# Five up-projection pairs per FFN layer in seven-product blocks, three down chunks of six, and retimed scheduler costs, in a two-layer hybrid decoder trunk

## The chip, the core and the metric

One NeuronCore of a Trainium2 chip runs the whole program. The metric is device time in microseconds of one execution; the time of a kernel is the median over its runs. TensorE is written PE, VectorE DVE, ScalarE ACT, GpSimd POOL, SyncE SP.

## What is computed

The trunk has two layers over 512 tokens of width 1024, all in float32. Layer 0 mixes with a Mamba-2 scan and a stick-breaking attention, layer 1 with an mLSTM; each layer then adds a gated convolutional FFN. The change is almost wholly in that FFN:

```python
def conv_ffn(h, up_w, conv_w, conv_b, down_w):
    u = causal_dwconv(h @ up_w, conv_w, conv_b)
    gate, val = jnp.split(u, 2, axis=-1)
    return (jax.nn.silu(gate) * val) @ down_w
...
        h = h + conv_ffn(rmsnorm(h, norm_w[layer, 1]), ffn_up_w[layer], ffn_conv_w[layer],
                         ffn_conv_b[layer], ffn_down_w[layer])
```

`up_w` is 1024 x 5632 (22 tiles of 128 gate columns, 22 of value columns), `down_w` is 2816 x 1024.

## The kernel before

Activations lie transposed, features on the 128 partitions and 512 tokens along the free axis: eight tiles of the residual `h`, each in a slot of a pool of 71 equal slots on chip. Every float32 product is made of three float32r products (`mm3`): each operand is split in a rounded part `hi` and a remainder `lo`, and hi*hi, hi*lo and lo*hi are summed in PSUM. ACT makes `hi` (a cast) and DVE makes `lo` (a subtraction), for the activations (`split`) and for every weight as it comes in from memory (`split_weights`). SP loads weights in "units" into two `raw` buffers; the split units stand in five `hi`/`lo` pairs (`W_BUFS`), so the makers of a unit wait until PE is done with the unit five before.

In `ffn` (line 1174) the step `("up", j)` is a pair: gate tile j and value tile 22+j. Each is eight weight tiles against eight token tiles (`feat`), 24 matmuls of 512 columns; then DVE scales by the norm (`u`), ACT and DVE make the three taps of the convolution (`c`), ACT the SiLU, DVE the product.

The down projection of the first 16 tiles is done by `down_blocks` (line 1227) in seven block products instead of eight (a Strassen-Winograd scheme on 2x2 blocks: two feature tiles by two halves of the tokens). For a pair of feature tiles, `token_sums` makes the token-side combinations (11, 21, 22, n1, n2, t3, t4) on DVE and splits them. On the weight side a block unit (`weight_tiles`) reads four blocks: the first two raw; two combinations `P1` and `P3` by a load from SP onto which a second DMA, issued by POOL, adds another block in flight; `P2` and `P4` by additions on DVE; the last raw. Seven products of 256 token columns run in three PSUM banks X, Z, Y, and DVE adds each finished partial sum to `h`, seven reads of 128x256 per pair of output tiles. The order is `FFN_PLAN`: chunks of eight tiles (`CHUNKS`) once their ups are done, and the last six tiles (`REST`) by plain products in `down_rest`.

The order of instructions is not the order of the code. All calls are recorded, and `Recorder.order` (line 318) makes a list schedule from them: each call has a cost in ns (`cost`), each pair of engines a latency, and pools of slots and buffers hold a call back until the right earlier tile is free. Each engine then runs its list strictly in turn. A cost thus changes no instruction, but which stands ahead of which, in the whole program.

Of the kernel before, what the change touches and what calls it, by code (L numbers as in the profile page):

```python
# [15 lines left out]
F32 = mybir.dt.float32  # L16
# [6 lines left out]
P = 128  # L23
# [61 lines left out]
def _ffn_units(i, l):  # L85
# [3 lines left out]
    for kind, n in FFN_PLAN:  # L89
        if kind == "up":  # L90
# [6 lines left out]
        else:  # L97
# [175 lines left out]
class Recorder:  # L273
# [15 lines left out]
    def cost(c):  # L289
# [25 lines left out]
        return 60 + 2.0 * n  # L315
# [129 lines left out]
SLOTS = 71  # L445
# [3 lines left out]
class Net:  # L449
# [724 lines left out]
    def ffn(self, l, h, last):  # L1174
        nc = self.nc
        xs, _, _, rb = self.norm(h, f"nw{l}1")
        pairs, ss, first = {}, [], None
        for kind, j in FFN_PLAN:
            if kind == "down":
                a, b = CHUNKS[j]  # L1180
                for c in range(4):
                    self.down_blocks([pairs[k] for k in range(a // 2, b // 2)], h, c)
# [4 lines left out]
            cc = []  # L1187
            for part in range(2):
                n = j + part * FF
                ps = self.ps(("pj", "zz", "yy")[self.n % 3])  # L1190
                self.feat(ps, xs)
                u, c = self.slot("u"), self.slot("c")
                nc.vector.tensor_tensor(u, ps, rb, op=ALU.mult)
                nc.scalar.activation(c, u, AF.Identity, scale=self.param(f"fw{l}2", n), bias=self.param(f"fb{l}", n))
                for d in (1, 2):
                    nc.vector.scalar_tensor_tensor(c[:, d:T], u[:, 0 : T - d], self.param(f"fw{l}{2 - d}", n), c[:, d:T],
                                                   op0=ALU.mult, op1=ALU.add)
                cc.append(c)
            nc.scalar.activation(cc[0], cc[0], AF.Silu)
            nc.vector.tensor_tensor(cc[1], cc[0], cc[1], op=ALU.mult)  # L1200
# [7 lines left out]
    def token_sums(self, c1, c2):  # L1208
# [275 lines left out]
```

## Time and profile before

| what | us |
|---|---|
| median of 3 runs (1389.22 to 1389.76) | 1389.6 |
| the profiled execution | 1389.56 |
| its span, first to last instruction | 1387.8 |
| PE busy | 1376.7 (99%) |
| DVE busy | 1116.2 (80%) |
| ACT busy | 783.9 (56%) |
| POOL busy | 87.1 (6%) |

Layer 0's FFN runs from about 452 to 808 us of the span, layer 1's from about 1027 to the end. A busy share of PE counts overlapped, modelled ends of its matmuls; how far apart they start is read from the chain of waits, where a run of n matmuls on the path has a length.

### The profile page before, as it was taken

The numbers are of one execution on the slowest core, as the hardware profiler recorded it, in microseconds if no ns is written. First come the engines' busy times: TensorE is split into PE (matmuls) and PEld (weight loads), VectorE is DVE, ScalarE is ACT, GpSimd is POOL, SyncE is SP. The second block draws the span as 40 slices with busy tenths as digits, with TensorE's granted clock in tenths as the row PEclk, the third lists the DMA queues.
The fourth block names the chain that finished last, engine by engine and source line by source line (L and its number), as shares of the span: only waits on it lengthen the run. The fifth ranks groups of instructions, "written<-read, shape, count | busy, mean of one in ns | idle before, by whom it ended". The sixth has DMA issues, their size and how long they took to land.

```text
span 1387.8 us, 20206 instructions
## 1 busy us (share of the span) xinstructions
PE 1376.7 (99%) x7491; PEld 1185.3 (85%) x7491; DVE 1116.2 (80%) x1963; ACT 783.9 (56%) x1325; POOL 87.1 (6%) x172
## 2 busy tenths in 40 slices
PE   9999999999999999999999999999999999999998
PEld 8898998989788888988898898888888899889887
DVE  7999889999997778878877657798758886888662
ACT  7798997786665444344434446776434444444440
POOL 0000001201120001000100000110000010010000
PEclk9999999999999999999999999999999999999999
DMA  6423223223312345243532225222234354443422
GB/s 220 130 77 112 86 78 98 70 83 132 98 46 91 101 127 137 92 138 113 129 122 95 81 82 171 77 92 89 65 106 126 102 129 129 122 133 95 137 68 84
DMA packets 53617, 147.96 MB, mean 107 GB/s; under 512 B 6136, under 2 KB 7160, under 8 KB 53520
## 3 DMA queue, kind: packets, MB, share of 16 engines
q1 hardware_dynamic: 48912, 138.29, 31.4%
q0 software_dynamic: 4608, 8.39, 3.7%
q8 instruction: 59, 0.97, 0.3%
q14 instruction: 38, 0.31, 0.1%
HBM read 141.36 MB, written 2.15 MB: 103 GB/s over the span
## 4 chain that ended last, share of the span: by engine, by line
PE 88%; DVE 5%; issue 3%; ACT 3%; POOL 1%; DMA 0%; SPq 0%; DVEq 0%; POOLq 0%; ACTq 0%
PE pj L436 43%; PE yy L436 26%; PE zz L436 14%; PE tt L436 5%; DVE gt L436 1%; DVE wt L436 1%; DVE lo L436 1%; DVE wTl L436 0%; ACT L436 0%; ACT Kh L436 0%; DMA h<-in_xT 0%; POOL wt L436 0%; ACT Q L436 0%; DVE ss L436 0%; ACT hi L436 0%
## 5 line engine op out<-in xcount | busy, mean ns | idle before, releaser
L436 ACT CAST hi<-raw 128x1024 fp32r<-128x1024 f32 (+2 forms) x236 | 227.8, 968 | 257.2 <-PE yy L436 58.6
L436 DVE TENSOR_TENSOR lo<-raw,hi 128x1024 fp32r<-128x1024 f32 (+2 forms) x236 | 263.8, 1120 | 25.2 <-ACT hi L436 24.5
L436 PE MATMUL pj<-xnh,hi 128*128 128x512 f32 x488 | 194.1, 398 | 0.0
L436 PE MATMUL pj<-xnh,lo 128*128 128x512 f32 x488 | 193.9, 397 | 0.0
L436 PE MATMUL pj<-xnl,hi 128*128 128x512 f32 x488 | 193.5, 396 | 0.0
L436 DVE SCALAR_TENSOR_TENSOR c<-u,pp,c 128x511 f32<-128x511 f32 (+2 forms) x212 | 158.0, 748 | 3.9 <-ACT c L436 1.6
L436 PE MATMUL yy<-xnl,hi 128*128 128x512 f32 x320 | 126.4, 395 | 0.0
L436 PE MATMUL yy<-xnh,lo 128*128 128x512 f32 x320 | 126.2, 394 | 0.0
L436 PE MATMUL yy<-xnh,hi 128*128 128x512 f32 x320 | 125.6, 392 | 0.0
L436 PE MATMUL pj<-lo,xnh 128*128 128x384 f32 (+2 forms) x320 | 108.6, 340 | 0.0
L436 PEld LDWEIGHTS pj<-xnh,lo 128*128 128x128 f32 x488 | 91.8, 188 | 19.1
L436 PEld LDWEIGHTS pj<-xnl,hi 128*128 128x128 f32 x488 | 91.8, 188 | 18.9
L436 PEld LDWEIGHTS pj<-xnh,hi 128*128 128x128 f32 x488 | 91.9, 188 | 18.8 <-issue 0.2
L436 PE MATMUL pj<-hi,xnl 128*128 128x384 f32 (+2 forms) x320 | 107.2, 336 | 0.0
L436 PE MATMUL pj<-hi,xnh 128*128 128x384 f32 (+2 forms) x320 | 106.8, 338 | 0.0
L436 ACT ACTIVATE c<-u,pp 128x512 f32<-128x512 f32 x100 | 81.1, 813 | 9.7 <-DVE u L436 8.3
L436 PE MATMUL zz<-xnl,hi 128*128 128x512 f32 x184 | 72.7, 395 | 0.0
L436 PE MATMUL zz<-xnh,lo 128*128 128x512 f32 x184 | 72.5, 394 | 0.0
L436 PE MATMUL zz<-xnh,hi 128*128 128x512 f32 x184 | 72.2, 392 | 0.0
L436 PEld LDWEIGHTS yy<-xnh,hi 128*128 128x128 f32 x320 | 60.2, 188 | 14.0
L436 PEld LDWEIGHTS yy<-xnl,hi 128*128 128x128 f32 x320 | 60.1, 188 | 13.9
L436 PEld LDWEIGHTS yy<-xnh,lo 128*128 128x128 f32 x320 | 60.1, 188 | 13.3
(418 smaller groups left out, 3330.7 us busy)
## 6 DMA issues: line engine op xcount, KB each, us to landing
raw<-in_w SPq DMA_DIRECT2D x168, 512.0 KB, 3.4
raw<-in_w SPq DMA_DIRECT2D x44, 384.0 KB, 3.1
P<-in_w SPq DMA_DIRECT2D x32, 256.0 KB, 5.6
P<-in_w POOLq DMA_DIRECT2D x32, 256.0 KB, 6.8
h<-in_xT SPq DMA_DIRECT2D x16, 256.0 KB, 4.7
E<-acsd SPq DMA_DIRECT2D x16, 256.0 KB, 3.9
raw<-in_w SPq DMA_DIRECT2D x16, 256.0 KB, 3.1
raw<-in_w SPq DMA_DIRECT2D x8, 264.0 KB, 2.7
```

Source lines behind the costliest of these rows:

```text
L436: getattr(getattr(nc, c.engine), c.method)(*(r(a) for a in c.args), **{k: r(v) for k, v in c.kw.items()})
```

## The change

Each FFN layer makes ups 7, 10, 13, 16 and 19 with the seven-product scheme: the two output tiles are gate and value tile, the four inner block pairs are the eight feature tiles of the normed input. The token-side combinations of the input (`xb`) are made once per layer, in four steps `("x", k)` between the first ups, from `h` times the norm weight (`hw`). The seven products per block (`blocks`, shared with the down projection) are gathered from PSUM to `u1` and `u2` by ACT (four of seven) and DVE (three), and then scaled. The down chunks are three of six tiles, with `REST` 18. There are 72 slots instead of 71. The scheduler's costs are changed for PE's products, DVE's scans, POOL's powers and masks. `SLOT` and all other constants stand.

```diff
-        if kind == "up":
+        if kind == "up" and n in UP_BLOCKS:
+            u.append(np.stack([up[m][:, k::2] for m in (n, FF + n) for k in range(2)], axis=1))
...
-CHUNKS = [(0, 8), (8, 16)]
-REST = 16
-FFN_PLAN = [("up", j) for j in range(9)] + [("down", 0)] + [("up", j) for j in range(9, 17)] + [("down", 1)]
-FFN_PLAN += [("up", j) for j in range(17, FF)] + [("rest", 0)]
+
+CHUNKS = [(0, 6), (6, 12), (12, 18)]
+REST = 18
+UP_BLOCKS = (7, 10, 13, 16, 19)
+FFN_PLAN = [("up", 0), ("up", 1), ("x", 0), ("up", 2), ("x", 1), ("up", 3), ("x", 2), ("up", 4), ("x", 3), ("up", 5)]
+FFN_PLAN += [("up", 6), ("down", 0)] + [("up", j) for j in range(7, 12)]
+FFN_PLAN += [("up", 12), ("down", 1)] + [("up", j) for j in range(13, 18)]
+FFN_PLAN += [("up", 18), ("down", 2)] + [("up", j) for j in range(19, FF)] + [("rest", 0)]
...
-                return max(n / 2.4 + 2.5, m * 0.84)
-            return max(4 * n / 2.4 + 5, 3.4 * m)
+                return max(n * 0.4414 + 5, m * 0.84)
+            return max(4 * n * 0.4414 + 5, 3.4 * m)
         if c.engine == "vector":
             rate = 0.52 if c.method == "tensor_scalar" and not psum else 1.042
             if c.method == "reciprocal":
                 rate = 6.2
+            if c.method == "tensor_tensor_scan":
+                rate = 2.04
...
-        return 60 + 2.0 * n
+        if c.method == "tensor_tensor":
+            return 250 + 190 * n
+        return 330 + 0.6 * n if c.method == "affine_select" else 100
...
-SLOTS = 71
+SLOTS = 72
...
-            r1, r2 = self.raw_tile(), self.raw_tile()[:, 0:kb]
+            r1, r2 = self.raw_tile()[:, 0 : 2 * kb], self.raw_tile()[:, 0:kb]
             self.nc.sync.dma_start(r1, src[:, 0 : 2 * kb])
-            p1, p2, p3, p4 = (self.slot(f"P{k}") for k in (1, 2, 3, 4))
+            p1, p2, p3, p4 = (self.slot(f"P{k}", n=kb) for k in (1, 2, 3, 4))
...
+            if kind == "x":
+                hw = []
+                for k in (2 * j, 2 * j + 1):
+                    hw.append(self.slot("hw"))
+                    v.tensor_scalar(hw[-1], h[k], self.param(f"nw{l}1", k), None, op0=ALU.mult)
+                xb.append(self.token_sums(*hw, xs[2 * j], xs[2 * j + 1]))
+                continue
...
+            us, cc = [None, None], []
+            if j in UP_BLOCKS:
+                us = self.up_blocks(xb, rb, j)
...
+                n, u, c = j + part * FF, us[part], self.slot("c")
+                if u is None:
+                    ps = self.ps(("pj", "zz", "yy")[self.n % 3])
+                    self.feat(ps, xs)
+                    u = self.slot("u")
+                    v.tensor_tensor(u, ps, rb, op=ALU.mult)
...
+    def token_sums(self, c1, c2, s1=None, s2=None):
...
+        half = lambda t, s: (t[0][:, s], t[1][:, s])
+        if s1 is None:
+            t = self.slot("B11", F32R)
+            self.nc.scalar.copy(t[:, a], c1[:, a])
+            v.tensor_tensor(t[:, b], c1[:, a], t[:, a].bitcast(F32), op=ALU.subtract)
+            s11, s2 = (t[:, a], t[:, b]), self.split(c2, "s")
+        else:
+            s11 = half(s1, a)
...
+    def blocks(self, xs, c, read):
...
         kb, n = len(xs) * P, T // 2
...
+        steps = (X, "11", "X1"), (Z, "21", "Z"), (X, "n2", "X2"), (Y, "n1", "Y1"), (X, "t3", "X3"), (Y, "22", "Y2"), (X, "t4", "X4")
+        for i, (ps, form, name) in enumerate(steps):
...
+    def up_blocks(self, xs, rb, c):
+        nc, v = self.nc, self.nc.vector
+        a, b = slice(0, T // 2), slice(T // 2, T)
+        u1, u2 = self.slot("u"), self.slot("u")
+        def read(name, ps):
+            if name in ("X1", "X2"):
+                nc.scalar.copy(u1[:, a if name == "X1" else b], ps)
+            elif name in ("Y1", "X4"):
+                nc.scalar.activation(u2[:, b if name == "Y1" else a], ps, AF.Copy, scale=-1.0)
+            elif name == "X3":
+                v.tensor_tensor(u2[:, b], u2[:, b], ps, op=ALU.subtract)
+            else:
+                o = u1[:, a if name == "Z" else b]
+                v.tensor_tensor(o, o, ps, op=ALU.add)
+        self.blocks(xs, c, read)
+        for u in (u1, u2):
+            v.tensor_tensor(u, u, rb, op=ALU.mult)
+        return u1, u2```

Three places in the instruction lists. On PE, where layer 0 reaches the end of the first down chunk (names: `F`, `s`, `G` the token-side forms of the FFN's activations, `xnh`/`xnl` the split input, `hi`/`lo` a weight unit; the number tells tiles apart). Before, PE goes from the down products to an ordinary up of 512 columns:

```order
L436 MATMUL pj_6638<-sh_6168,hi_6539 128x256
L436 MATMUL pj_6638<-sl_6181,hi_6539 128x256
L436 MATMUL pj_6638<-sh_6168,lo_6550 128x256
L436 MATMUL yy_6686<-xnh_5207,hi_6599 128x512
L436 MATMUL yy_6686<-xnl_5240,hi_6599 128x512
```

Of the change, it goes to up 7, of 256 columns:

```order
L446 MATMUL pj_6459<-Fh_6057,hi_6354 128x256
L446 MATMUL pj_6459<-Fl_6072,hi_6354 128x256
L446 MATMUL pj_6459<-Fh_6057,lo_6379 128x256
L446 MATMUL yy_6489<-xnh_5200,hi_6441 128x256
L446 MATMUL yy_6489<-xnl_5232,hi_6441 128x256
L446 MATMUL yy_6489<-xnh_5200,lo_6468 128x256
```

The first product of up 7 ("11") takes the split input itself and stands between products of the down chunk.

On DVE, the norm ahead of layer 0's FFN, from the remainder of the sum of squares (`accl`) to the first `u`. Before:

```order
L436 TENSOR_TENSOR accl_5438<-acc_5220,acch_5429 128x512
L436 TENSOR_TENSOR lo_5446<-raw_5401,hi_5435 128x1024
L436 TENSOR_SCALAR var_5457<-tt_5441 128x4
L436 COPY rep_5467<-rstd_5463 128x512
L436 TENSOR_TENSOR u_5489<-pj_5387,rb_5481 128x512
```

Of the change:

```order
L446 TENSOR_TENSOR accl_5465<-acc_5213,acch_5454 128x512
L446 TENSOR_SCALAR hw_5473<-h_4054,pp 128x512
L446 TENSOR_TENSOR lo_5481<-raw_5402,hi_5467 128x1024
L446 TENSOR_SCALAR var_5491<-tt_5463 128x4
L446 TENSOR_TENSOR Gl_5493<-G_5457,Gh_5477 128x512
L446 TENSOR_SCALAR hw_5502<-h_4064,pp 128x512
L446 TENSOR_TENSOR F_5505<-hw_5473 128x256
L446 SCALAR_TENSOR_TENSOR F_5505<-hw_5502,F_5505 128x256
L446 COPY rep_5512<-rstd_5498 128x512
L446 TENSOR_TENSOR Fl_5526<-F_5505,Fh_5515 128x512
L446 TENSOR_TENSOR u_5538<-zz_5415,rb_5529 128x512
```

The token-side sums of the input now stand between the variance, its power on POOL (`rstd`) and the first use of the norm.

On SP, and on DVE which waits for it, the loads of the `P` tiles. Before, around the first down chunk of layer 0:

```order
L436 DMA P_1276_5700<-in_w 128x512
L436 DMA P_1278_5706<-in_w 128x512
L436 DMA raw_5738<-in_w 128x1024
L436 DMA raw_5776<-in_w 128x1024
L436 DMA raw_5830<-in_w 128x1024
L436 DMA raw_5867<-in_w 128x1024
L436 DMA raw_5912<-in_w 128x1024
L436 DMA raw_5949<-in_w 128x1024
```

Of the change, around the third chunk of layer 0:

```order
L446 DMA raw_8176<-in_w 128x768
L446 DMA P_1684_8211<-in_w 128x384
L446 DMA P_1686_8233<-in_w 128x384
L446 DMA raw_8246<-in_w 128x384
L446 DMA P_1701_8257<-in_w 128x384
L446 DMA P_1703_8314<-in_w 128x384
L446 DMA raw_8357<-in_w 128x768
L446 DMA P_1718_8372<-in_w 128x384
```

Before, this unit's P loads stood six raw loads ahead of its own first raw load (raw_5949); now they stand right behind it (raw_8176 belongs with P_1684 and P_1686), and the next unit's follow. On DVE, the stretch that ends with the addition that needs P_1684; of the change:

```order
L446 TENSOR_TENSOR Fl_8224<-F_8157,Fh_8215 128x512
L446 SCALAR_TENSOR_TENSOR G_8202<-F_8157,c_8171 128x256
L446 SCALAR_TENSOR_TENSOR c_8221<-u_8209,pp,c_8221 128x511
L446 TENSOR_TENSOR lo_8240<-raw_8089,hi_8207 128x384
L446 SCALAR_TENSOR_TENSOR c_8221<-u_8209,pp,c_8221 128x510
L446 TENSOR_TENSOR Gl_8251<-G_8202,Gh_8236 128x512
L446 TENSOR_TENSOR u_8268<-zz_8204,rb_5529 128x512
L446 TENSOR_TENSOR lo_8275<-raw_8176,hi_8260 128x768
L446 TENSOR_TENSOR h_4016<-h_4016,pj_8262 128x256
L446 SCALAR_TENSOR_TENSOR c_8281<-u_8268,pp,c_8281 128x511
L446 TENSOR_TENSOR P_1685_8312<-P_1684_8211,raw_8176 128x384
```

The numbers of tiles rise in the order in which the list schedule takes calls up, so a load numbered 8211 is taken up while DVE stands between u_8209 and P_1685_8312; before, 44 instructions of DVE lay between P_1276_5700 and the addition that reads it (P_1277_6016).

## Rows read from the trace of the kernel before

**Rows 1.** The page, busy time of each engine: busy us, share of the span, instructions.
```profile
PE 1376.7 (99%) x7491; PEld 1185.3 (85%) x7491; DVE 1116.2 (80%) x1963; ACT 783.9 (56%) x1325; POOL 87.1 (6%) x172
```

**Rows 2.** Chain that ended last, whole span: start us, us, what, matmuls in the piece.
```profile
462.99 73.59 PE pj L436 x318
...
561.56 1.42 PE zz L436 x12
...
732.94 11.11 PE yy L436 x48
...
789.86 4.16 PE tt L436 x18
```

**Rows 3.** Busy time by stretch, both FFNs and the mixers of both layers.
```profile
core 0: us, PE busy (x) PEld busy (x) DVE busy (x) ACT busy (x) POOL busy (x), PEclk, DMA share, GB/s
200.00:420.00 220.00, 216.30 (x1266) 189.65 (x1264) 207.13 (x391) 158.67 (x310) 36.27 (x65) 1.00 0.28 85
...
452.00:808.00 356.00, 356.00 (x1874) 304.20 (x1873) 276.31 (x420) 159.11 (x223) 16.52 (x41) 1.00 0.39 112
...
812.00:1030.00 218.00, 216.57 (x1162) 182.80 (x1161) 166.80 (x373) 128.37 (x250) 15.99 (x41) 1.00 0.32 101
1027.00:1387.00 360.00, 357.16 (x1878) 304.77 (x1877) 266.05 (x405) 147.25 (x204) 15.30 (x17) 1.00 0.38 112
```

**Rows 4.** Waits, whole span: engine, line, waited for, us, times, longest us.
```profile
ACT hi L436 <- PE yy L436: 71.1, 47, 3.8
```

**Rows 5.** DVE in order of time, two idle times of layer 0's FFN.
```profile
461.23 0.43 DVE L436 COPY rep<-rstd 128x512 f32<-128x512 f32 x1 [1.12 <-POOL rstd L436]
...
598.79 0.69 DVE L436 TENSOR_TENSOR u<-yy,rb 128x512 f32<-128x512 f32 x1 [2.52 <-PE yy L436]
```

**Rows 6.** DVE, 452 to 808 us, groups by form: busy us, mean ns, idle before.
```profile
L436 DVE TENSOR_TENSOR lo<-raw,hi 128x1024 fp32r<-128x1024 f32 x48 | 58.7, 1222 | 7.0 <-ACT hi L436 7.0
...
L436 DVE TENSOR_TENSOR lo<-P,hi 128x512 fp32r<-128x512 f32 x32 | 21.7, 687 | 2.0 <-ACT hi L436 1.9
...
L436 DVE TENSOR_TENSOR u<-pj,rb 128x512 f32<-128x512 f32 x21 | 14.5, 691 | 19.3 <-PE pj L436 17.2 <-ACT rb L436 2.0
...
L436 DVE TENSOR_TENSOR h<-h,pj 128x256 f32<-128x256 f32 x28 | 11.7, 419 | 6.7 <-PE pj L436 6.1
...
L436 DVE TENSOR_TENSOR lo<-raw,hi 128x768 fp32r<-128x768 f32 x8 | 7.6, 956 | 0.1
```

**Rows 7.** DVE in order of time, 480 to 485 us: start us, us, instruction.
```profile
480.26 0.42 DVE L436 TENSOR_TENSOR G<-c,c 128x256 f32<-128x256 f32 x1
480.60 0.42 DVE L436 SCALAR_TENSOR_TENSOR G<-F,c 128x256 f32<-128x256 f32 x1
...
482.13 1.22 DVE L436 TENSOR_TENSOR lo<-raw,hi 128x1024 fp32r<-128x1024 f32 x1
483.27 0.69 DVE L436 TENSOR_TENSOR Fl<-F,Fh 128x512 fp32r<-128x512 f32 x1
483.87 0.69 DVE L436 TENSOR_TENSOR Gl<-G,Gh 128x512 fp32r<-128x512 f32 x1
```

**Rows 8.** ACT, 452 to 808 us, groups by form.
```profile
L436 ACT CAST hi<-raw 128x1024 fp32r<-128x1024 f32 x48 | 50.5, 1051 | 68.9 <-PE yy L436 27.9 <-PE pj L436 22.4 <-DMA raw<-in_w 15.6
...
L436 ACT CAST hi<-P 128x512 fp32r<-128x512 f32 x32 | 18.8, 617 | 23.1 <-PE pj L436 7.3 <-PE yy L436 7.2 <-issue 6.2
...
L436 ACT CAST B<-c 128x256 fp32r<-128x256 f32 x8 | 3.2, 402 | 7.0 <-DVE c L436 7.0
```

**Rows 9.** DMA issues, 452 to 808 us: KB each, median us from issue to landing.
```profile
raw<-in_w SPq DMA_DIRECT2D x47, 512.0 KB, 3.4
P<-in_w SPq DMA_DIRECT2D x16, 256.0 KB, 5.3
P<-in_w POOLq DMA_DIRECT2D x16, 256.0 KB, 6.6
```

**Rows 10.** PE, whole span, groups by form: busy us, mean ns of one.
```profile
L436 PE MATMUL pj<-xnh,hi 128*128 128x512 f32 x488 | 194.1, 398 | 0.0
...
L436 PE MATMUL pj<-Fh,hi 128*128 128x256 f32 x64 | 18.1, 282 | 0.0
```

More of the change, by code (lines that the diff above doesn't have):

```diff
@@ L96, in _ffn_units @@
             u += [x.reshape(P, 4, (b - a) // 2, P) for x in t]
-        else:
+        elif kind == "rest":
             u += _feat(dn[REST * P :])
     return u
-CHUNKS = [(0, 8), (8, 16)]
-REST = 16
-FFN_PLAN = [("up", j) for j in range(9)] + [("down", 0)] + [("up", j) for j in range(9, 17)] + [("down", 1)]
-FFN_PLAN += [("up", j) for j in range(17, FF)] + [("rest", 0)]
+CHUNKS = [(0, 6), (6, 12), (12, 18)]
[5 more added lines that the diff above has]
+FFN_PLAN += [("up", 18), ("down", 2)] + [("up", j) for j in range(19, FF)] + [("rest", 0)]
 X = lambda kind, *ns: [(kind, n) for n in ns]
@@ L1174, in ffn @@
     def ffn(self, l, h, last):
-        nc = self.nc
+        nc, v = self.nc, self.nc.vector
         xs, _, _, rb = self.norm(h, f"nw{l}1")
-        pairs, ss, first = {}, [], None
+        pairs, ss, first, xb = {}, [], None, []
         for kind, j in FFN_PLAN:
+            if kind == "x":
[5 more added lines that the diff above has]
+                continue
             if kind == "down":
@@ L1181, in ffn @@
                 for c in range(4):
-                    self.down_blocks([pairs[k] for k in range(a // 2, b // 2)], h, c)
+                    self.down_blocks([pairs[k] for k in range(a // 2, b // 2)], h[2 * c], h[2 * c + 1], c)
                 continue
@@ L1222, in token_sums @@
         gs = self.split(g, "G")
-        half = lambda t, s: (t[0][:, s], t[1][:, s])
-        return {"11": (t[:, a], t[:, b]), "21": half(s2, a), "22": half(s2, b),
+        return {"11": s11, "21": half(s2, a), "22": half(s2, b),
                 "n1": half(fs, a), "n2": half(fs, b), "t3": half(gs, a), "t4": half(gs, b)}
-    def down_blocks(self, xs, h, c):
-        v = self.nc.vector
+    def blocks(self, xs, c, read):
         kb, n = len(xs) * P, T // 2
-        a, b = slice(0, n), slice(n, T)
         X, Z, Y = (self.ps(t)[:, 0:n] for t in (("pj", "yy", "zz"), ("yy", "pj", "pj"))[c % 2])
-        h1, h2 = h[2 * c], h[2 * c + 1]
-        at = {"i": 0, "u": None}
-        def product(ps, form, more=False):
-            i = at["i"]
+        steps = (X, "11", "X1"), (Z, "21", "Z"), (X, "n2", "X2"), (Y, "n1", "Y1"), (X, "t3", "X3"), (Y, "22", "Y2"), (X, "t4", "X4")
+        for i, (ps, form, name) in enumerate(steps):
             if i % 2 == 0:
-                at["u"] = self.unit()
-            hi, lo = at["u"]
-            at["i"] = i + 1
+                hi, lo = self.unit()
+            more = name[1:] > "1"
             for k, x in enumerate(xs):
@@ L1247, in product, with down_blocks, read @@
                 self.mm3(ps, (hi[:, s], lo[:, s]), x[form], not more and k == 0, k == len(xs) - 1, skip_group_check=more)
-        add = lambda o, ps, op=ALU.add: v.tensor_tensor(o, o, ps, op=op)
-        product(X, "11")
-        product(Z, "21")
-        add(h1[:, a], X)
-        product(X, "n2", True)
-        add(h1[:, a], Z)
-        product(Y, "n1")
-        add(h1[:, b], X)
-        product(X, "t3", True)
-        add(h2[:, b], Y, ALU.subtract)
-        product(Y, "22", True)
-        add(h2[:, b], X, ALU.subtract)
-        product(X, "t4", True)
-        add(h1[:, b], Y)
-        add(h2[:, a], X, ALU.subtract)
+            read(name, ps)
+    def down_blocks(self, xs, h1, h2, c):
+        a, b = slice(0, T // 2), slice(T // 2, T)
+        to = {"X1": h1[:, a], "Z": h1[:, a], "X2": h1[:, b], "Y2": h1[:, b], "Y1": h2[:, b], "X3": h2[:, b], "X4": h2[:, a]}
+        def read(name, ps):
+            op = ALU.add if name in ("X1", "Z", "X2", "Y2") else ALU.subtract
+            self.nc.vector.tensor_tensor(to[name], to[name], ps, op=op)
+        self.blocks(xs, c, read)
+    def up_blocks(self, xs, rb, c):
+        nc, v = self.nc, self.nc.vector
+        a, b = slice(0, T // 2), slice(T // 2, T)
+        u1, u2 = self.slot("u"), self.slot("u")
+        def read(name, ps):
+            if name in ("X1", "X2"):
[7 more added lines that the diff above has]
+                v.tensor_tensor(o, o, ps, op=ALU.add)
+        self.blocks(xs, c, read)
+        for u in (u1, u2):
+            v.tensor_tensor(u, u, rb, op=ALU.mult)
+        return u1, u2
     def down_rest(self, ss, h, last):
         nc = self.nc
-        for c in range(8):
+        for c in range(KD):
             ps = self.ps(("pj", "zz", "yy", "tt")[c % 4])
```

18 lines of the change are left out of this document (4 added, 14 removed).

## Prediction

> **What bounds the kernel now.** First the busy times: PE 99%, DVE 80%, ACT 56% [rows 1]. PE's number alone proves little, since overlapped matmuls count as busy; so next the chain of waits, for the pace at which matmuls start [rows 2]. In the FFN 318 matmuls of 512 columns take 73.59 us and 48 take 11.11, which is 0.2314 us each; 12 of 256 columns take 1.42, or 0.1183. Now the whole of a layer's FFN by this pace: 22 pairs x 48 x 0.2314 = 244.4; eight down blocks x 84 x 0.1183 = 79.5; eight rests of 4.16 = 33.3 [rows 2]; 357.2 in all. The stage takes about 356 [rows 3]. So in the FFN PE never waits, and matmul work taken away there is time taken away, as long as the makers keep up. They do so with room: DVE is busy 276.3 of 356 us, ACT 159.1 [rows 3], and the casts of weights wait for PE to free a buffer [rows 4], as DVE waits for finished products (2.5 us in one case [rows 5]). The mixers have little idle PE: 3.7 us and 1.4 us in two stretches that hold them [rows 3]. The granted clock is 1.00 in each stretch, which is the level of 2.4 GHz, and an FFN as dense as before gives no cause for another.
>
> **PE, the gain.** A pair done plainly costs 48 x 0.2314 = 11.11; in blocks 7 products x 4 blocks x 3 = 84 matmuls of 256 columns, 9.94. That is 1.17 less. Per layer five up pairs and, since the chunks cover 18 tiles instead of 16, one more down pair (84 small ones for 48 large over the four output pairs): 6 x 1.17 = 7.0; two layers: 14.0. All of it lies on the path. The number of weight loads rises by 36 per pair, 432 in all, but the pace of 0.1183 was measured with a load before each matmul.
>
> A rule that speaks against this: the Trainium skill, "TensorE: Matmul & The Clock Gate", section Back-to-back issue gap, gives a sustained 131 ns per matmul at 512 columns and 81 ns at 128. By it a half-width matmul costs much more than half, and an estimate of some 98 ns at 256 makes a block pair 8.2 us against 6.3 plain, so the change would lose near 2 us per pair; the rows here, 231 and 118 ns for float32r, do not bear it out.
>
> **DVE, what is added.** The durations of DVE's groups [rows 6] overlap by some 0.085 us; what an instruction occupies is read from start to start [rows 7]: 0.60 for 512 columns (483.27 to 483.87), 1.14 for 1024, 0.34 for 256; by the same overlap 0.87 for 768 [rows 6] and 0.47 for 384, between its neighbours.
> Up pair in blocks: the splits become 1.14 + 5 x 0.60 = 4.14 instead of 2 x 1.14 = 2.28; two additions for P2 and P4, 1.20; three reads of PSUM, 1.01; the scaling stays at two of 0.60. +4.1, five times: +20.4.
> Input forms: four steps of two `hw`, four half-width sums and two remainders: 4 x (0.68 + 1.36 + 1.20) = +13.0. For `hw` no row shows the operation; the nearest are the one-input copy of 512 columns at 0.43 less overlap [rows 5] and a two-input one at 0.60, so 0.34 to 0.60; I take 0.34, as it has one tensor operand; the other end adds 2.
> Down: a block is 0.87 + 5 x 0.47 + 2 x 0.47 + 7 x 0.34 = 6.5, twelve of them 78; before 1.14 + 7 x 0.60 + 2.35 = 7.7, eight of them 61.5: +16.5. Rest: eight splits of 512 for 768, -2.2. One more pair in token sums, 3.5 for 1.2: +2.3.
> Sum +50 per layer: 326 of an FFN that would last 349. ACT [rows 8] gains some 30: a block pair 1.05 + 5 x 0.62 + 4 x 0.40 = 5.7 for 2.1, five times 18; eight casts of forms, 5; twelve smaller down blocks for eight, 7. That is 189 of 349, covered by its idle time.
>
> **Does DVE keep ahead?** Cover is the lead of the split units over PE. Summed by the two lists from the last out-projection on, DVE and PE then run equal, near 100 us each, until the end of the first down chunk: seven plain pairs at 8.5 us of DVE against 11.1 of PE give 18 us, which the forms (13) and the norm's rest use up. At a block pair DVE needs 12.5 against 9.9 of PE, but the plain pairs between give 2.6 back each, and a down block needs 6.5 against 7.5. The lead swings most where large units give way to small ones: by the running sums it falls 13.6 us into the first chunk, and before it fell 13.4 at the same place without an idle PE. I cost DVE's load at nothing; the cover left is some 23 us of idle DVE per layer. If it goes, PE waits for `lo` right behind ups 7, 10, 13.
>
> **The P tiles.** The forms hold 16 slots through up 19. With split input 16, `h` 8, `rb` 1 and a chunk's pairs 3 x 7 = 21, that is 62 of 72; before 16 + 8 + 1 + 28 = 53 of 71. So P tiles are called up later. A P tile needs its SP load and then POOL's, 5.3 + 6.6 = 11.9 us [rows 9] (they are 256 KB; those of the down blocks now have 192). In the lists the cover from SP's place to DVE's addition was 16 to 31 us for all but each chunk's second unit (6 to 7.5, where SP could run ahead); now it is 7.4 to 9.4 for the second unit of a chunk, 8.8 to 9.6 for those behind it in the third chunk, 11 to 17 elsewhere. What is short of 11.9 sums to some 22 us per layer, 13 of it in the third chunk. It first eats the lead: four units of 2.1 us of PE, some 8. What gets through is bounded by 0 below and 5 per layer from this chunk, 7 with the others. I take 1 per layer, +2, nearer the lower end since smaller loads land sooner and DVE has its idle time.
>
> A rule of the Trainium skill bears on this: "SBUF — State Buffer", section SBUF: two separate sides, has a DVE copy or scaling from SBUF to SBUF lock GpSimd out of writing its DMA descriptors while it runs. No row shows it yet, and by it an estimate of the loss is one `hw`, a third of a us, for a load of POOL that meets it.
>
> **Rescheduling.** The other cost edits change no instruction. They can win back at most PE's idle time in the mixers, some 5 us [rows 3]; from the other side, moved waits can cost as much. DVE fills 207 of 220 us in layer 0's attention, so neither is likely large; I take 0. On the norm DVE waited 1.1 us for POOL's power [rows 5], where sums of the input forms now stand; that is off PE's path.
>
> **Sum**, against the profiled execution's own 1389.56 (span 1387.8; the median of the runs is 1389.6, the same): 1389.56 - 14.0 + 2 + 0 = 1377.6. The 0.2% that a measurement of this kernel can tell from no change is 2.8 us, so faster means below 1386.8 and slower above 1392.4.
>
> **Rivals.**
> 1. Nothing gets through: leads cover all late P tiles and the truer costs win back 4 us in the mixers: 1389.6 - 14 - 4 = 1371.6. For it: PE waits for almost nothing now. Against: the P tiles' cover of 7 to 9 us. Chance 0.15.
> 2. DVE becomes the bound. Of its 80 us of idle time in layer 0's FFN, only part vanishes when it runs late: waits for PE do; those for ACT's `hi` (7.0 and 1.9 [rows 6]), for POOL and in dependent chains do not. If 35 us per layer stay, a layer takes 326 + 35 = 361, and the gain is gone or nearly: about 1387 to 1391. For it: 93% of load. Against: ACT has room. Chance 0.06.
> 3. Slower: SP sends its loads in turn, so a P load that waits for a slot holds the raw load behind it, and PE, ACT and DVE run dry together. If the whole shortfall of 22 us per layer reaches PE the time is 1389.6 - 14 + 44 = 1420; it is slower than before from 17 of the 44 on, at some 1393. For it: raw loads now stand between P loads, and 10 free slots where 18 were. Against: PE's lead at each chunk. Chance 0.05.
> 4. The narrow matmuls do not come at half the pace, the mechanism behind the sustained figures weighed above. By the durations of single matmuls, 0.282 against 0.398 [rows 10], a pair would be 23.7 against 19.1, twelve of them +55: 1445. The pace itself can be read [rows 2], so 0.01.
> That the change does not do what it says is excluded by the lists: PE has 432 more matmuls, those of up 7 at 256 columns.
>
> **How the numbers follow.** The forecast, 1373 to 1385 with 1377.6 as the likeliest, has the remaining 0.73. Range 1371 to 1387: all of it, nearly all of rival 1, and the lower edge of rival 2. Faster: 0.73 + 0.15 + 0.01 of rival 2 = 0.89; same 0.05; slower 0.06.
>
> **What would show it.** PE: blocks of 12 matmuls in 1.42 us in the ups too, and an FFN of 349 to 352 us with PE's waits still near nothing; if PE waits for `lo` or `hi` right after a down chunk begins, the P tiles are late, and then DVE's P additions wait for a DMA. DVE some 325 us busy per FFN. A time above 1387 with an undisturbed PE would mean that the pace of 256 columns or the count was wrong; the same with an idle PE in the FFN, rival 2 or 3, told apart by whether DVE is busy or waits.

## The result and the profile after

The changed kernel takes 1403.39 us (median of 5 runs, 1398.99 to 1409.17) against 1389.52 of the kernel before on the same chip: ratio 1.0105, 95% interval 1.0074 to 1.0136. It is slower by about 1%; the forecast was 1377.6, faster. The profiled execution is the slowest of the five, 1409.17 us and 31.6 more than the forecast; its trace is read for where these went. Of all executions here one, in experiment 9, ran at a granted clock of 0.75 (1651.5 us); the ratio there leaves it out.

Busy time of each engine in the changed kernel (answers to [rows 1]), and the chain of work that ended last, by engine:

```profile
PE 1379.3 (98%) x7923; PEld 1204.1 (86%) x7923; DVE 1199.3 (85%) x2249; ACT 829.3 (59%) x1470; POOL 121.0 (9%) x208
...
PE 68%; DVE 17%; DMA 7%; ACT 4%; issue 3%; SPq 0%; DVEq 0%; ACTq 0%
```

The same chain of the kernel before:

```profile
PE 88%; DVE 5%; issue 3%; ACT 3%; POOL 1%; DMA 0%; SPq 0%; DVEq 0%; POOLq 0%; ACTq 0%
```

PE's busy share says almost nothing; the chain does. Now a quarter of it runs through DVE and DMA. By stretch (answers to [rows 3]):

```profile
core 0: us, PE busy (x) PEld busy (x) DVE busy (x) ACT busy (x) POOL busy (x), PEclk, DMA share, GB/s
200.00:420.00 220.00, 219.33 (x1290) 195.45 (x1289) 204.58 (x387) 155.86 (x302) 36.05 (x62) 1.00 0.27 85
452.00:824.00 372.00, 360.12 (x2115) 317.43 (x2114) 314.88 (x553) 182.45 (x295) 32.71 (x59) 0.99 0.45 119
824.00:1040.00 216.00, 213.77 (x1135) 177.96 (x1135) 168.15 (x384) 126.91 (x248) 16.11 (x41) 1.00 0.32 102
1040.00:1404.00 364.00, 356.80 (x2095) 313.40 (x2093) 303.65 (x534) 171.19 (x276) 31.30 (x35) 0.99 0.45 123
```

Both FFNs became longer, and DVE is not full in them. How much is pace and how much is standing still comes from the starts of PE's matmuls in the trace: for each one, the distance to the next start less the undisturbed distance (231 ns at 512 columns, 118 at 256). A stage runs from its norm's first matmul to the next one's (the last to the final matmul):

```
us                                layer 0's FFN      layer 1's FFN
                                  before   after     before   after
length                             357.6   372.8      353.0   359.4
all starts at undisturbed pace     356.7   351.9      352.2   345.4
gaps over 0.4 us                     0.0   13.4 (10)    0.0    7.9 (7)
60 to 130 ns over the pace           0.3    5.8         0.3    3.7
```

So the gain is there: 4.8 and 6.8 us of pace (in layer 0 some of the next mixer's products lie within the stage). It is outweighed by 17 standstills, which the kernel before does not have, and by stretches in which each matmul comes some 100 ns late; what the rows leave, 1.7 and 2.4 us, are delays of other sizes. Three pieces of the chain:

```profile
495.31 11.16 PE zz L446 x48
...
600.95 2.58 PE pj L446 x12
...
608.12 1.42 PE pj L446 x12
```

A plain half pair of 48 and twelve narrow matmuls have the durations of [rows 2]; but right behind the standstills at 594.5 (1.3 us) and 598.7 (2.1 us) the same twelve take 2.58 us. The granted clock shows why:

```profile
586.00:592.00 6.00, 6.00 (x28) 4.88 (x27) 6.00 (x11) 3.74 (x8) 0.19 (x1) 1.00 0.47 153
599.00:605.00 6.00, 4.06 (x22) 4.05 (x22) 4.35 (x7) 4.20 (x7) 0.00 (x0) 0.72 0.30 101
...
1339.00:1345.00 6.00, 3.19 (x17) 2.69 (x16) 4.17 (x8) 3.13 (x5) 0.00 (x0) 0.76 0.29 89
```

Behind some standstills, part of the next microseconds runs at the lower level of 1.2 GHz: at four places in the FFNs, near 601, 700, 762 and 1342 us, and not behind the others. In sum the standstills are paid 1.4 times: 21.3 us of gaps, and 9.0 us of slow matmuls (9.5 less the 0.5 of before), most of them at these places. What the engines waited for (us, times, longest; answers to [rows 4]), first ACT and DVE, which make what PE needs, then PE itself:

```profile
ACT hi L446 <- DMA raw<-in_w: 88.9, 53, 5.4
...
DVE P L446 <- DMA raw<-in_w: 18.4, 11, 3.6
...
PE pj L446 <- ACT u L446: 6.6, 5, 1.9
PE yy L446 <- ACT hi L446: 3.6, 2, 2.2
PE yy L446 <- DVE h L446: 3.0, 4, 0.8
PE yy L446 <- DVE lo L446: 2.8, 4, 1.0
```

From the kernel before:

```profile
ACT hi L436 <- DMA raw<-in_w: 55.1, 34, 4.1
```

DVE's P additions did not wait there at all. Of the 17 standstills eight ended on a split weight (five `lo`, three `hi`) and nine on a late read of PSUM (five `u` by ACT, four `h` by DVE). One standstill in full: the chain from 592 us on, and behind it the three rows (ACT, DVE, SP in order of time) that led to it:

```profile
591.89 0.98 ACT hi L446
592.88 6.62 DMA raw<-in_w
...
599.58 1.04 ACT hi L446
600.62 0.28 ACT u L446
```

```profile
587.38 0.60 ACT L446 CAST hi<-raw 128x512 fp32r<-128x512 f32 x1
...
592.13 0.68 DVE L446 TENSOR_TENSOR lo<-raw,hi 128x512 fp32r<-128x512 f32 x1
...
592.88 3.35 SPq L446 DMA_DIRECT2D raw<-in_w  x2
```

Only two raw buffers exist. One was held until DVE, busy without a gap, came to its `lo` 4.1 us after the cast; the next load was issued then, and landed 6.6 us later, where 3.4 was the median before [rows 9]. DMA from 592 to 600 us, by queue (packets, MB, share of the 16 engines' time), and the two raw loads' landing:

```profile
q1 hardware_dynamic: 285, 1.04, 35.9%
q0 software_dynamic: 288, 0.39, 30.9%
...
raw<-in_w SPq DMA_DIRECT2D x2, 512.0 KB, 5.7
```

The second line is POOL's accumulating loads (each adds a block onto what the tile holds): with 0.39 MB they take nearly as much of the DMA engines' time as 1.04 MB of plain loads, some 2.3 times as much per byte. Whether this, the buffers, DVE's queue or the new order makes the loss is what the runs were for. **Theory A**: weights that pass the two raw buffers come late. **Rivals**: the new durations spread the whole order badly (B); the up blocks alone do it (C); DVE's queue is late and the loads only follow (D).

### The profile page after: what moved, and what is told of

Its sections match the earlier page's. It is cut to its first block, busy times and chain, and to the rows that moved or that the text cites. A ratio compares the mean times of both kernels' runs of the same rounds, so it can differ in the third digit from the quotient of the medians.

```text
span 1407.5 us, 21738 instructions
## 1 busy us (share of the span) xinstructions
PE 1379.3 (98%) x7923; PEld 1204.1 (86%) x7923; DVE 1199.3 (85%) x2249; ACT 829.3 (59%) x1470; POOL 121.0 (9%) x208
## 3 DMA queue, kind: packets, MB, share of 16 engines
q1 hardware_dynamic: 56400, 141.44, 31.6%
q0 software_dynamic: 9792, 14.68, 6.9%
## 4 chain that ended last, share of the span: by engine, by line
PE 68%; DVE 17%; DMA 7%; ACT 4%; issue 3%; SPq 0%; DVEq 0%; ACTq 0%
PE pj L446 37%; PE yy L446 15%; PE zz L446 11%; DMA raw<-in_w 7%; PE tt L446 5%; DVE lo L446 4%; DVE c L446 3%; DVE h L446 2%; ACT hi L446 1%; DVE P L446 1%; DVE u L446 1%; DVE gt L446 1%; ACT c L446 1%; DVE wt L446 1%; DMA E<-mrow 0%
## 5 line engine op out<-in xcount | busy, mean ns | idle before, releaser
L446 ACT CAST hi<-raw 128x1024 fp32r<-128x1024 f32 (+3 forms) x252 | 225.3, 898 | 234.3 <-DMA raw<-in_w 88.9
L446 DVE TENSOR_TENSOR lo<-raw,hi 128x1024 fp32r<-128x1024 f32 (+3 forms) x252 | 259.3, 1030 | 53.7 <-ACT hi L446 50.1
L446 PE MATMUL pj<-xnh,hi 128*128 128x512 f32 (+1 forms) x552 | 212.9, 386 | 0.1
L446 PE MATMUL pj<-xnh,lo 128*128 128x512 f32 (+1 forms) x552 | 211.9, 384 | 0.0
L446 PE MATMUL pj<-xnl,hi 128*128 128x512 f32 (+1 forms) x552 | 211.7, 384 | 0.0
L446 DVE SCALAR_TENSOR_TENSOR c<-u,pp,c 128x511 f32<-128x511 f32 (+2 forms) x212 | 157.4, 746 | 7.7 <-ACT c L446 6.6
L446 PEld LDWEIGHTS pj<-xnh,hi 128*128 128x128 f32 x552 | 103.9, 188 | 19.9 <-ACT u L446 1.1
L446 PEld LDWEIGHTS pj<-xnl,hi 128*128 128x128 f32 x552 | 104.1, 189 | 19.3
L446 PEld LDWEIGHTS pj<-xnh,lo 128*128 128x128 f32 x552 | 103.8, 188 | 19.6 <-issue 0.2
L446 PE MATMUL pj<-hi,xnh 128*128 128x384 f32 (+2 forms) x320 | 107.6, 339 | 0.0
L446 PE MATMUL pj<-lo,xnh 128*128 128x384 f32 (+2 forms) x320 | 107.3, 337 | 0.0
L446 PE MATMUL pj<-hi,xnl 128*128 128x384 f32 (+2 forms) x320 | 107.2, 337 | 0.0
L446 ACT ACTIVATE c<-u,pp 128x512 f32<-128x512 f32 x100 | 81.2, 814 | 41.4 <-DVE u L446 40.2
L446 POOL DMA_DIRECT2D P<-in_w x68 | 60.2, 995 | 519.7 <-DMA P<-in_w 210.6
L446 ACT CAST hi<-P 128x384 fp32r<-128x384 f32 (+1 forms) x136 | 70.3, 541 | 48.6 <-PE zz L446 14.9
L446 PE MATMUL zz<-xnh,lo 128*128 128x512 f32 (+1 forms) x208 | 80.8, 389 | 0.0
L446 PE MATMUL zz<-xnl,hi 128*128 128x512 f32 (+1 forms) x208 | 80.6, 388 | 0.0
L446 PE MATMUL zz<-xnh,hi 128*128 128x512 f32 (+1 forms) x208 | 80.6, 387 | 0.0
L446 DVE TENSOR_TENSOR lo<-P,hi 128x384 fp32r<-128x384 f32 (+1 forms) x136 | 78.7, 591 | 0.0
L446 PE MATMUL yy<-xnh,hi 128*128 128x512 f32 (+1 forms) x192 | 72.3, 376 | 3.6 <-ACT hi L446 3.6
L446 PE MATMUL yy<-xnh,lo 128*128 128x512 f32 (+1 forms) x192 | 72.5, 378 | 1.6 <-DVE lo L446 1.6
L446 PE MATMUL yy<-xnl,hi 128*128 128x512 f32 (+1 forms) x192 | 71.8, 374 | 0.0
## 6 DMA issues: line engine op xcount, KB each, us to landing
raw<-in_w SPq DMA_DIRECT2D x142, 512.0 KB, 3.4
raw<-in_w SPq DMA_DIRECT2D x26, 256.0 KB, 2.9
P<-in_w SPq DMA_DIRECT2D x20, 256.0 KB, 4.2
P<-in_w POOLq DMA_DIRECT2D x20, 256.0 KB, 5.8
```

Source lines behind the costliest of these rows:

```text
L446: getattr(getattr(nc, c.engine), c.method)(*(r(a) for a in c.args), **{k: r(v) for k, v in c.kw.items()})
```

## The experiments

Every ratio is to the kernel before, run beside it on the same chip, with its 95% interval.

**1. The scheduler's durations alone**, in the kernel before (the three cost edits of the diff ahead, nothing else).

> The kernel before with nothing but the scheduler's new durations. Theory A (the loss is made in the new FFN: weights that pass the two raw buffers come late there, and PE stalls): the order of the two mixers and of the old FFN is about as good as it was, 1389.5 us within 4. Rival B (the new durations spread the whole program's order badly): most of the loss is here already, 1400 us or more, with PE gaps of over 0.4 us in the FFN, of which the kernel before has none.

1392.62 us, ratio 1.0024 (1.0014 to 1.0033). Layer 0's FFN is 4.9 us longer with two gaps of 1.2 and 0.9 us; what lies ahead of it is 3 us shorter. So the new order costs 3 us by itself; rival B falls for the rest.

**2. The change with the durations of before** (the cost edits undone).

> The changed kernel with the scheduler's durations of before. Theory A: the same two raw buffers and the same order of loads, so stalls of the same kind and size or more: 1400 to 1415 us. Rival B (the new durations are the loss): the forecast comes back, about 1376 to 1380 us.

1399.36 us, 1.0076 (1.0059 to 1.0093), a hair under theory A's range; the standstills are there (14 over 0.4 us in the FFNs). B's 1376 to 1380 is out.

**3. The chunks without the up blocks.**

```diff
-UP_BLOCKS = (7, 10, 13, 16, 19)
+UP_BLOCKS = ()
```
(with the plan's `x` steps dropped and each down chunk right behind its last pair)

> The changed kernel with its three chunks of 6 and 72 slots, but without the up blocks and without the block sums of x for them. By the matmuls alone: 84 more of 256 columns at 0.118 us and 48 fewer of 512 at 0.2314 us in each layer, so 1.2 us less per layer, 1387.2 us. Theory A: a block group of a chunk of 6 keeps PE for 63 x 0.118 = 7.4 us and not 9.9, and its raw tiles must come round as often: the stalls that lie in the down chunks of the changed kernel (553, 656, 742, 750, 1143, 1240 and 1332 us, 5.8 us in all) stay, the others go: 1390 to 1396 us. Rival C (the up blocks alone make the loss): no PE gap over 0.4 us in the FFN, 1386 to 1388 us.

1388.71 us, 0.9991 (0.9982 to 1.0000), no FFN gap over 0.4 us: near rival C's numbers, and my reading that seven of the standstills belong to the smaller down chunks was wrong. ACT waits 82.2 us for raw tiles here too, yet PE never stands: the lead that the chunks alone leave covers these waits. It fits what experiment 8 finds: the chunks alone bring the accumulating loads of layer 0's FFN from 4.20 to 4.72 MB, the up blocks bring them to 7.34. The up blocks with the old chunks of eight would hold 69 of the 72 slots by the prediction's counts (53 and 16); that half was not tried.

**4. A third raw buffer.**

```diff
-RAW_BUFS = 2
-SLOTS = 72
+RAW_BUFS = 3
+SLOTS = 71
```

> The changed kernel with a third raw buffer, and 71 slots in place of 72 to pay for it. Theory A: the stalls whose chain ends in a raw load go, about 14 of the 21 us of stalls and with them half or more of the 10 us at the lower clock: 1378 to 1388 us. Rival D (VectorE's in-order queue is what is late, and the loads only follow it): the four stalls at the first up block behind a down chunk (594, 697, 1184, 1281 us) stay and others take the place of those at the loads: 1395 to 1405 us.

1397.13 us, 1.0056 (1.0038 to 1.0073): rival D's range, but not its mechanism. ACT's wait for raw tiles falls to 18.2 us and the four standstills that D kept go as well; instead there are six, of other places and sizes (2.7 us at 554, 4.5 at 1325). The chain into the longest, and DVE in order of time:

```profile
1316.58 1.34 DVE lo L446 x2
...
1318.01 7.72 DMA P<-in_w
...
1326.36 0.55 DVE lo L446
```

```profile
1325.75 0.69 DVE L446 TENSOR_TENSOR P<-P,raw 128x512 f32<-128x512 f32 x1 [5.35 <-DMA P<-in_w]
```

Now DVE stands 5.35 us in front of a P addition until an accumulating load lands, 7.7 us after its issue; the `lo` and `h` work behind it, ready long before, waits too. The scheduler reckons 4.5 us for such a load, so it puts the addition too early. Hence **theory A'**: the order is made with DMA times that the new traffic does not keep.

**5, 6 and 9. The durations that the scheduler gives to DMAs**, together and one by one, in the changed kernel with its two buffers.

```diff
-                end = start + 2000 + cost
+                end = start + 3000 + cost
             elif c.method == "dma_start":
-                end = start + 4500
+                end = start + 6500
```

Both:

> The changed kernel, two raw buffers and 72 slots as it has them; only the two durations that the scheduler gives to DMAs are longer: 3000 ns and not 2000 ahead of a load's bytes, 6500 and not 4500 for an accumulating load (in the changed kernel's FFN an accumulating load of 256 KB lands in 5.7 us by the median, and the 512 KB raw load ahead of the stall at 598.7 us landed after 6.6 us where the scheduler reckons 3.5). Theory A' (an instruction that is put into VectorE's or ScalarE's queue too early stands there until its tile lands, and what is ready behind it frees no raw buffer and reads no PSUM): stalls over 0.4 us in the FFN fall from 21 us to under 8, and with them the stretches at the lower clock: 1377 to 1386 us. Rival E (two raw buffers can't carry three streams, in whatever order): 1395 to 1405 us.

Only the accumulating loads':

> Of the two durations of the run with both, only that of the accumulating loads is longer (6500 and not 4500). If these loads are what the queues wait for, the gain of both is here: 1378 to 1386 us. If it is the raw loads that pass the two buffers (in the changed kernel ScalarE waits 89 us for raw tiles, VectorE 18), most of the loss stays: 1394 to 1403 us.

Only the plain loads':

> Of the two longer DMA durations only that of the plain loads (3000 ns ahead of the bytes and not 2000; the accumulating loads as in the changed kernel, 4500). Both together gave 1386.1 us, the accumulating loads' alone 1409.6, no gain. If the raw loads' duration is the whole of it: 1384 to 1389 us. If it takes both (the accumulating loads' only counts once the raw loads are placed right): 1390 to 1398 us.

| durations | us | ratio (95%) |
|---|---|---|
| as in the change | 1403.39 | 1.0105 (1.0074 to 1.0136) |
| accumulating loads 6500 | 1409.63 | 1.0134 (1.0116 to 1.0152) |
| plain loads 3000 | 1386.55 | 0.9975 (0.9961 to 0.9990) |
| both | 1386.08 | 0.9965 (0.9951 to 0.9979) |

One number in the scheduler, a plain load's lead, is worth 17 us and turns the sign; the other gains nothing with two buffers. Both together leave 9.8 us of FFN gaps where theory A' allowed 8, and a time just past its range. The loads did not become faster: 512 KB take 3.9 us in layer 0's FFN by the median, as in the changed kernel. What changed is the order, and with it ACT's wait for raw tiles (67.7 us with both, 88.9 in the changed kernel); that it is the work standing behind an unlanded tile is argued, not shown. Rival E falls.

**7. Both cures**: three raw buffers, 71 slots, durations 2500 and 6500.

> Three raw buffers and 71 slots, and the scheduler's DMA durations longer (2500 and 6500). With three raw buffers the stalls that were left were VectorE's: it stood in front of a P addition for up to 5.4 us until an accumulating load landed (7.7 us after its issue), with sums into h and lo halves ready behind it. Theory A': these go, under 6 us of FFN stalls: 1375 to 1383 us. Rival F (VectorE, at 86% of the span, has no room to catch up, wherever the addition stands): 1390 to 1397 us as with three buffers alone.

1382.77 us, 0.9950 (0.9936 to 0.9965), in the range of theory A' (FFN gaps 3.6 us in all, expected under 6). ACT's wait for raw tiles is 14.3 us of the changed kernel's 88.9. Rival F is out.

**8. The accumulating loads' bytes.** The changed kernel's order, instruction for instruction, with narrow sums; the kernel leaves out the rest of each sum and only its time counts (so too in 13, 14, 16 and 17):

```diff
-                self.nc.gpsimd.dma_start(p, src[:, i * kb : (i + 1) * kb], accum_op=ALU.add)
+                self.nc.gpsimd.dma_start(p[:, 0:8], src[:, i * kb : i * kb + 8], accum_op=ALU.add)
```

> The changed kernel in its own order, instruction for instruction; each accumulating load adds 8 columns in place of all of its block's 384 or 512, so the sums of the weight blocks are left out but for these columns. It prices the bytes of the accumulating loads. Theory G (their bytes crowd out the raw loads that are under way beside them): raw loads of 512 KB land in under 3.5 us where they took up to 6.6, and most stalls go: 1380 to 1390 us. Theory A' alone (the place in the queues is what hurts, the transfers are only as long as the scheduler left no room for) expects a part, since the accumulating loads themselves land sooner: 1388 to 1398 us. If neither: 1399 to 1407 us.

1379.49 us, 0.9930 (0.9915 to 0.9944), better than theory G asked for: all the loss is gone, with the order, two buffers and 2000/4500 untouched, and the time is within 2 us of the forecast. Landing of raw loads from 452 to 815 us, shortest, median, longest, of the changed kernel and then of this run:

```profile
DMA to landing us min/median/max: 2.4/3.4/7.1
```

```profile
DMA to landing us min/median/max: 2.3/3.2/4.6
```

POOL's queue from 452 to 815 us (packets, MB, share of the 16 engines' time), of the changed kernel and then of this run:

```profile
q0 software_dynamic: 4896, 7.34, 13.3%
```

```profile
q0 software_dynamic: 4896, 0.14, 2.1%
```

The number of packets is the same, so it is not the issuing of these loads that costs, but their bytes; and the order is only bad for the times that these bytes make. But this takes away two things, their share of the DMA engines and the P tiles' own wait.

**13, 14, 16 and 17. The bytes without the wait.** Narrow sums as in 8, and behind them, into tiles that nothing reads, the rest of the bytes; each with a control in which these spare loads are 8 columns wide (`m = 8`).

```diff
+            for i in (3, 0):
+                m = min(kb - 8, 496)
+                self.nc.gpsimd.dma_start(self.spare[i // 3][:, 0:m], src[:, i * kb + 8 : i * kb + 8 + m], accum_op=ALU.add)
```

> As the run in which each accumulating load adds 8 columns (1379.5 us), but behind the two of a block tile two more accumulating loads of 496 columns at most go into spare tiles that nothing reads: the bytes are back, and no P tile waits for them. 71 slots in place of 72 pay for the spare tiles, so the order is not quite that one's. The sums of the weight blocks are left out but for 8 columns. If the bytes hurt by crowding out the raw loads: 1390 to 1402 us, and 8 us or more over the run with narrow spare loads in the same order. If they hurt only because the P tiles themselves came late: within 3 us of that run.

> The control: the same order of instructions, the spare accumulating loads narrowed to 8 columns. Whatever theory holds, near the run with 8 columns alone: 1378 to 1384 us.

1398.77 us (1.0067, 1.0047 to 1.0087) and 1377.41 (0.9910, 0.9895 to 0.9925), the expected difference at the wrong place: the FFNs are alike (354.2 and 354.1, 348.4 and 348.0), what lies ahead of layer 0's FFN is 19 us longer. Nothing held the spare loads back, so POOL issued them all in the first 184 us. The pair tells nothing of the FFN. Second try, each spare load recorded as a reader of its P tile:

> The first run with spare accumulating loads lost its 21 us in the first mixer, not in the FFN (354.2 and 348.4 us, as its control): nothing held those loads back, and GpSimd had issued all of them long before the block tiles. Here the scheduler takes each one as a reader of the P tile that it goes with, so that it stands right behind the two narrow loads of its block tile; on the chip it waits for nothing but the spare tile. The sums of the weight blocks are again left out but for 8 columns. If the bytes hurt by crowding out the raw loads: 8 us or more over the run with narrow spare loads, 1386 to 1400 us, in FFN stalls whose chains end in raw loads. If they hurt only because the P tiles came late: within 3 us of that run.

> The control in the same order, the spare loads narrowed to 8 columns: 1376 to 1384 us by either theory.

1391.66 us (1.0014, 0.9996 to 1.0032) and 1377.84 (0.9915, 0.9900 to 0.9930): 13.8 us for bytes that nothing waits for. Waits and DMA issues (452 to 815 us) of the one, then of the control:

```profile
ACT hi L446 <- DMA raw<-in_w: 93.2, 63, 4.5
...
DVE P L446 <- DMA raw<-in_w: 13.7, 8, 2.7
```

```profile
q0 software_dynamic: 9792, 7.30, 14.9%
...
raw<-in_w SPq DMA_DIRECT2D x34, 512.0 KB, 3.9
```

```profile
ACT hi L446 <- DMA raw<-in_w: 58.7, 51, 3.5
...
DVE P L446 <- DMA raw<-in_w: 2.0, 3, 0.8
```

```profile
q0 software_dynamic: 9792, 0.28, 4.2%
...
raw<-in_w SPq DMA_DIRECT2D x33, 512.0 KB, 3.4
```

The raw waits of the changed kernel are back, and standstills of up to 1.5 us with them, as the theory of crowding out expected. In all eight waits of the P additions the P tile's own load had landed 3.9 us or more before the raw tile. The greater part, 13.8 of the 24 us that experiment 8 gives back, is the crowding out of the raw loads. Where the other 10 come from is open: the spare loads are somewhat narrower, with an order of their own, and POOL itself waited 10.6 us for their tiles. The P tiles' own lateness, which is what experiment 4 shows with three buffers, does not show with two: in all eleven waits of the changed kernel's P additions the accumulating load had landed 2.7 to 9.1 us before the raw tile.

**10, 11 and 12. No accumulating loads.** B2 and B3 are loaded once each, and POOL adds out of SBUF; two raw buffers (10), three (11), three and eight up pairs (12). The scheduler gives plain loads 3000 ns in 10 and 2500 in 11 and 12, and POOL's sums a duration of their own.

```diff
-            for p, i in ((p1, 3), (p3, 0)):
-                self.nc.sync.dma_start(p, src[:, 2 * kb : 3 * kb])
-                self.nc.gpsimd.dma_start(p, src[:, i * kb : (i + 1) * kb], accum_op=ALU.add)
+            r2 = self.slot("r2", n=kb)
+            self.nc.sync.dma_start(p3, src[:, 2 * kb : 3 * kb])
+            self.nc.sync.dma_start(r2, src[:, 3 * kb : n])
+            self.nc.gpsimd.tensor_tensor(p1, p3, r2, op=ALU.add)
+            self.nc.gpsimd.tensor_tensor(p3, p3, r1[:, 0:kb], op=ALU.add)
```

> The changed kernel with two raw buffers and 72 slots, the plain loads' longer duration (3000), and no accumulating loads: B2 and B3 are loaded once each into slots (four block loads per block tile in place of seven), and GpSimd makes P1 = B2 + B3 and P3 = B2 + B0 out of SBUF. Theory G (the accumulating loads' time on the DMA engines is what made the raw loads and the P tiles late): no FFN stall over 1 us, 1374 to 1381 us, 5 us or more under the run with both longer durations. Rival H (GpSimd's sums are slow, or hold up VectorE's reads and writes of the same SBUF): VectorE's mean times per instruction grow or its P additions wait for GpSimd, 1386 to 1400 us.

> The same GpSimd sums with a third raw buffer, 71 slots, and 2500 for the plain loads. If the raw buffers still bound once the accumulating loads are gone, this is 2 us or more faster than with two; if not, it is the same within 1.5 us: 1374 to 1380 us either way.

> The run with GpSimd sums and three raw buffers, and eight up pairs per layer in block products in place of five (7, 9, 11, 13, 15, 17, 19, 20). If PE's pace is all that counts once the loads are on time, three more pairs in each of two layers at 1.17 us give 7 us: 1367 to 1374 us. Rival I (VectorE, some 90% busy in the FFN with five, becomes the bound): 1374 to 1385 us, PE waiting for lo and h.

1393.99 (1.0031, 1.0018 to 1.0044), 1404.86 (1.0115, 1.0100 to 1.0130), 1407.77 (1.0129, 1.0112 to 1.0146): rival H in 10, and beyond all that was expected in 11 and 12. In 10 PE stands 18.1 us in the FFNs, most of it for DVE's `h`. POOL and DVE in order of time in 11:

```profile
1233.03 1.32 POOL L446 TENSOR_TENSOR P<-P,r 128x512 f32<-128x512 f32 x1 [5.95 <-DMA r<-in_w]
1234.43 1.49 POOL L446 TENSOR_TENSOR P<-P,raw 128x512 f32<-128x512 f32 x1
```

```profile
1232.29 0.55 DVE L446 TENSOR_TENSOR lo<-P,hi 128x384 fp32r<-128x384 f32 x1
...
1233.42 2.91 DVE L446 TENSOR_TENSOR lo<-P,hi 128x384 fp32r<-128x384 f32 x2
```

Two `lo` of 0.55 us each last 2.91, until 0.4 us after POOL's two sums are done. So it goes on: over the whole of 11 some 60 DVE instructions take over 0.3 us more than the median of their form, 43 us in all, and nearly all of them have both inputs in SBUF and overlap one of POOL's 68 sums (90 us).

**15. Six up pairs** on experiment 7, at other places: `UP_BLOCKS = (7, 9, 11, 13, 15, 17)`.

> The fastest version so far that computes everything (three raw buffers, 71 slots, DMA durations of 2500 and 6500; 1382.8 us) with six up pairs per layer in block products in place of five: 7, 9, 11, 13, 15, 17. By PE's pace one more pair in two layers gives 2.3 us: 1379 to 1382 us. If the accumulating loads of 8 more block tiles a layer crowd the DMA engines again, or VectorE has no room: 1383 to 1392 us.

1379.66 us, 0.9930 (0.9913 to 0.9947), in the first range: 3.1 less than with five pairs, for 2.3 by pace, though the two intervals overlap. By stretch:

```profile
452.00:808.00 356.00, 354.42 (x2169) 316.06 (x2168) 321.06 (x568) 187.31 (x305) 34.28 (x61) 1.00 0.48 127
1024.00:1374.00 350.00, 347.16 (x2113) 308.25 (x2111) 303.56 (x537) 172.82 (x279) 32.90 (x37) 1.00 0.47 127
```

DVE has 321 of 356 us, and PE hardly stands (four FFN gaps, 4.3 us): the fastest version that computes everything, and faster than both kernels.

## Why the prediction was wrong

- **PE's pace and count: right.** Twelve narrow matmuls in 1.42 us, 48 wide in 11.16, the stage's sum 6.8 us shorter in layer 1, where 7.0 was reckoned. With the accumulating bytes gone the whole kernel takes 1377.4 to 1379.5 (experiments 8, 14, 17). That this is the forecast of 1377.6 is part luck: these kernels leave out most of the sums, and the 2 us put down for late P tiles stand where 3.1 of rescheduling belong. Rival 4 falls.
- **DVE's load: right in size, and covered.** 314.9 us in layer 0's FFN for the 326 reckoned, and 321 with six pairs in experiment 15, where PE stood for 1.9 us of that FFN. Rival 2 falls.
- **Rescheduling, taken as 0 within 5:** +3.1 alone (experiment 1), inside its bounds, and not the 4 us won back of rival 1.
- **The P tiles, the step that failed.** "What gets through is bounded by 0 below and 5 per layer from this chunk, 7 with the others. I take 1 per layer, +2" asks only whether each P tile arrives in time. To that question the answer was better than reckoned: in layer 0's FFN the two loads of a P tile of 192 KB took 3.7 and 4.8 us by the median, 8.5 and not 11.9, and no P addition that waited had its own load land last. What the term left at nothing is what the additional loads do to the others. From 452 to 815 us the accumulating loads went from 4.20 to 7.34 MB and from 7.0 to 13.3% of the DMA engines' time (the views of experiment 8; POOL's queue and the landing of raw loads in the kernel before:)

```profile
q0 software_dynamic: 2304, 4.20, 7.0%
```

```profile
DMA to landing us min/median/max: 2.6/3.3/4.7
```

  The raw loads beside them, which this term does not mention, landed up to 7.1 us after issue instead of 4.7, and each passes one of two buffers that an engine's queue must free. The term was to hold some 24 us and not 2 (experiment 8), 13.8 of it by way of the raw loads (16 and 17). A DMA share of 0.39 on average [rows 3] looked like room; 592 to 600 us of the changed kernel shows a local two thirds.
- **Rival 3 had the sign but not the mechanism.** It put SP in front of P loads that wait for slots. Experiment 8 keeps SP's order and its slots and loses nothing: SP waits for a slot or buffer to be freed by a `lo` 655.2 us there and 655.0 in the changed kernel, by a P addition 141.4 and 143.2, so these waits are not the cause. "PE waits for `lo` or `hi`" came as written under what would show it for eight of the 17 standstills, but DVE's P additions waited for raw loads, not for P, until the third buffer.
- **The clock.** "An FFN as dense as before gives no cause for another" was right in its condition; when the density went, the 1.2 GHz stretches added 9 us.

## What to carry to other kernels

Price added DMA traffic by the DMA engines' time in its own stretch, accumulating loads apart from plain ones, and then ask which other loads pass there through few buffers. In a kernel with an order fixed ahead, the DMA lead that the scheduler assumes is a tuning constant as real as a buffer count: here 1000 ns of it, for plain loads, were worth 17 us. To tell bytes from order, shrink the transfers and keep every instruction.

## What the hardware showed

- POOL's accumulating loads cost the DMA engines 2.1 times a plain load's time per byte, over the changed kernel's span:

```profile
q1 hardware_dynamic: 56400, 141.44, 31.6%
q0 software_dynamic: 9792, 14.68, 6.9%
```

  Whether the adding, the queue or the smaller packets (1.5 and 2.5 KB) make it, no run separates. The Trainium skill, "DMA: Bandwidth & Descriptors", section Queues, rings and completion order, has each engine go round between its queues packet by packet; that fits plain loads slowed by a neighbour, though no run here shows the turns.
- A POOL sum of two SBUF tiles (128x512, 1.3 to 1.6 us) stops DVE's two-input instructions in SBUF, as far as the rows show for its whole length (2.91 us for two of 0.55). The Trainium skill, "SBUF — State Buffer", section Who interferes with whom, has a DVE instruction with two SBUF inputs contend with a GpSimd instruction that reads SBUF, one blocked for the whole of the other, and the trace agrees. The other direction, which the prediction weighed (DVE locking POOL out of its descriptors), no run here isolates; experiment 8 keeps all of POOL's loads and DVE's instructions and loses nothing, so it is not the loss here.
- The granted clock fell to 0.72 and 0.76 in the 6 us around standstills of 2.1 and 2.4 us; one of 2.1 us at 640.7 us was followed by no slow stretch (1.00 from 640.7 to 648).
